# A one-core mLSTM and sparse-attention block: the compression's first layer in fp32r with its parts side by side, block-by-block scaling in the first and last attention unit, and decays formed a step earlier

## The chip, the core and the metric

The kernel runs on one core of a Trainium2 chip. The metric is the device time of one execution in microseconds (us). Smaller is better.

## The reference

One decoder layer works on 512 tokens of width 1024. A normalised x goes through one input projection of 8448 columns. Its columns feed an mLSTM branch (4 heads of 256) and a sparse attention branch (8 query heads of 64 in 2 key groups). The merged branches go through an output projection, a residual and a last norm. All inputs are fp32. What this change touches:

```python
p = _split_in(hN @ w_in[l])
# compression of keys and of values: 31 overlapping blocks of 32 tokens, 2 groups
def _compress(kv, pos_emb, w1, w2):
    blocks = kv[:, idx] + pos_emb[None, None, :, None, :]
    blocks = jnp.moveaxis(blocks, 3, 1).reshape(B, G, n_cmp, CMP_BLOCK * dk)   # (1, 2, 31, 2048)
    return jax.nn.gelu(blocks @ w1) @ w2                                       # w1 2048x128, w2 128x64
# attention, per block of 128 queries
p_c = jax.nn.softmax(jnp.where(m_c, s_c, NEG), axis=-1) * m_c        # against compressed keys
p_s = jax.nn.softmax(s_s, axis=-1)                                   # selected blocks
p_w = jax.nn.softmax(jnp.where(m_w, s_w, NEG), axis=-1)              # window
return g[..., 0:1] * o_c + g[..., 1:2] * o_s + g[..., 2:3] * o_w
# mLSTM, per head
s = jnp.einsum('bhld,bhsd->bhls', qc, kc) * jnp.exp(logD - m_t[..., None])
h = num / jnp.maximum(jnp.abs(den), jnp.exp(-m_t))[..., None]
...
x = x + merged @ w_out[l]
return _rmsnorm(x, final_norm_g)
```

With 512 tokens, 8 selection blocks and 16 chosen ones, every selection block is chosen, so both the selected and the window branch are plain causal attention with their own keys and values.

## The kernel before, in words

**Projections.** Each fp32 operand that goes into a large product is split into two fp32r parts, a high part `h` and a rest `l`, and three products replace one: h·h, l·h and h·l. For a weight panel of 128x1024 the load is `wr`, ScalarE (ACT) writes `wh`, VectorE (DVE) subtracts and writes `wl`. One projection job (`cols`) is 24 matmuls `pp<-hTh,wh`, `pp<-hTl,wh`, `pp<-hTh,wl` of 128x512: 8 blocks of the width by 3 products. `cols(NKC, ..., 2)` cuts one such job into two token halves of 128x256.

**The stream.** Jobs stand in a queue, `stream`. `stream.step(n)` issues the next n matmuls of it, `stream.run(n)` finishes n jobs, and each finished job calls its `post` function. Matmuls of the stream are what TensorE (PE) does between the steps of the other work; this text calls them fill. They have to be done at some time, so moving them from one place to another changes no total.

**What sets the order.** Each engine has one queue, in order. A list scheduler makes it from the order in which the code is written; where an engine's name is in the set `ordered`, the written order holds: ACT and DVE while the first attention query is prepared, PE at the beginning and the end of the kernel. Loads are issued by SyncE (SP) in its queue's order. A tile pool's buffer comes free when its last reader ends.

**Compression.** `blocks(i)` (i = 0 keys, 1 values) loads the 2048x128 weight into `w1t`, copies the projection to `Z` and forms `X`, the overlapping blocks with the position term added. `hidden(i)` multiplies: 16 products in plain fp32, each 128x128 of `w1t` with 128x64 of `X`. The trace shows two records for each. Then comes the gelu chain `u`, `u2`, and `compress_k`, `compress_v` multiply by the second weight `w2t` and leave `KC` (keys) and `VC` (values). The tiles of this stage lie in the pool `cmp`, over memory that earlier tiles used.

**Attention.** `rope_a` copies a projected query or key and turns it by DMA (`rot`); `rope_b` and `query_heads` finish it and leave the parts `Th`. There are 16 units: 4 query pairs c, 2 heads hh, 2 branches b. `score` makes `ps<-k,Th` for the query blocks qb = 0 to 3 of 128, 256, 384 and 512 columns; `softmax_block` negates and masks on DVE (a custom instruction that leaves the row extreme in `st`), and takes exp on ACT with the row sum. At qb = 3 one reciprocal of four columns is multiplied by the gates and GpSimd (POOL) scales the four blocks of `P`. Then `P` is transposed on PE (`pt<-cst,P`), split (`pth`, `ptl`) and multiplied with the values (`po`). `tick(FILL)` puts 3 fills behind each step, `START_FILL` 12 behind each of the first unit's. `compressed(c)` makes the scores against `KC`: `pp<-KC,rh`, softmax `sc`, transposes `pp<-cst,sc`.

**mLSTM.** For each of 4 heads: the decay matrix `Dm` starts from `ps<-ghl,sel` and seven exps on ACT; the scores `ps<-qkh,qkh` are multiplied into it, split into `Sh`, `Sl`, multiplied with the values into `num`, normalised, and transposed (`pt<-cst,num`) into `yah`. Before the transposes the stream goes on until the next head's key is projected; after the last head `NORM_FILL` 30 fills stand there.

**End.** The sums of squares of each block of 128 tokens collect in `fs`; `begin`, `more` and `factor` on POOL add them in `fb` and raise to the power -1/2.

Of the kernel before, what the change touches and what calls it, by code (L numbers as in the profile page):

```python
# [60 lines left out]
def build(  # L61
# [731 lines left out]

    def blocks(i):
        def post(ps):
            w1, w2 = ((cmp_w1_k, cmp_w2_k), (cmp_w1_v, cmp_w2_v))[i]
            nc.sync.dma_start(W1[i], w1[0].rearrange("(j q) h -> q j h", q=128))
# [12 lines left out]
            pool.memset(X[:, :, :, 31:32], 0.0)  # L810
            for g in range(2):
                zz = Z[:, g, :]
                zin = bass.AP(zz.tensor, zz.offset, [zz.ap[0], [1, 16], [8, 31]])
                dve.tensor_tensor(
                    X[:, :, g, 0:31], zin,
                    cpos[:, i * 16 : i * 16 + 16].unsqueeze(2).broadcast_to([128, 16, 31]), OP.add,
                )
# [428 lines left out]
    for h in range(4):  # L1246
        for i in range(2):
            for e in range(2):
                conv(i, h, e)
    for j in range(ND):  # L1250
        branch(GB, j, ybh, ybl, 4)
    stream.run(4)
    values(0)

    for h in range(4):
        (qh, ql), (kh, kl) = qk[0, h], qk[1, h]
        vh, vl = vv[h]
# [86 lines left out]
    with tc.tile_pool(name="fin", bufs=1, reuse_waits="tile") as fp:  # L1344
# [112 lines left out]
        def more(tb, n):  # L1457
            v = fb[:, tb : tb + 1]
            keep(pool.tensor_tensor(v, v, fs[:, tb, n : n + 1], OP.add))
# [138 lines left out]
```

## Time and profile before

| what | value |
|---|---|
| time, median of three runs | 612.02 us (611.96, 612.02, 612.77) |
| the profiled execution's own time | 612.24 us |
| its span, first to last instruction | 610.4 us |
| PE busy | 596.2 us, 98% |
| DVE busy | 483.1 us, 79% |
| ACT busy | 343.2 us, 56% |
| POOL busy | 63.4 us, 10% |

The span is what the trace covers; the execution's own time has 1.8 us around it. "Busy" is the time in which at least one instruction of that engine is in flight. Matmuls overlap: a 128x512 matmul has a record of 0.39 us, and the next starts about 0.23 us after it, so PE's busy share hides short waits that the distance between the starts of two matmuls shows. Places below are given in us from the start of the span.

### The profile page before, as it was taken

How to read it: one execution, taken by the hardware profiler on the slowest of the kernel's cores; microseconds unless marked ns; L12 is line 12 of the kernel's file. 1: busy time of each engine (PE TensorE's matmuls, PEld its weight loads, DVE VectorE, ACT ScalarE, POOL GpSimd, SP SyncE). 2: the span in 40 equal slices, each digit the busy share in tenths (PEclk: the TensorE clock that was granted, in tenths of full speed). 3: DMA queues.
4: the chain of work that ended last, by engine and by line, in shares of the span. 5: the costliest groups of instructions: out<-in, count | busy, mean ns of one | idle time of the engine just before them, and what ended most of it. 6: DMA issues, size and time to landing. Idle time of an engine off the chain costs nothing. (4 is left out here: it accounts for less than half of the span.)

```text
span 610.4 us, 8577 instructions
## 1 busy us (share of the span) xinstructions
PE 596.2 (98%) x3008; PEld 499.5 (82%) x3008; DVE 483.1 (79%) x906; ACT 343.2 (56%) x635; POOL 63.4 (10%) x126
## 2 busy tenths in 40 slices
PE   8999999999999999999999999999999999999995
PEld 6988888888888877888888887888788878888884
DVE  5879798696686578886977684889898997589984
ACT  6854646664442356665765674465756563434564
POOL 3000000000100003222122131000000000010122
PEclk9999999999999999999999999999999999999998
DMA  7966555302068361323313113422242234890633
GB/s 221 349 162 190 183 168 160 116 2 86 18 185 207 78 173 46 97 59 86 81 47 103 53 34 122 138 70 70 69 130 80 89 87 131 301 253 18 208 52 139
DMA packets 83637, 74.18 MB, mean 122 GB/s; under 512 B 5197, under 2 KB 65225, under 8 KB 83594
## 3 DMA queue, kind: packets, MB, share of 16 engines
q1 hardware_dynamic: 82296, 70.94, 39.1%
q0 software_dynamic: 1008, 2.36, 2.1%
q8 instruction: 24, 0.39, 0.3%
q10 hardware_dynamic: 290, 0.33, 0.2%
q14 instruction: 19, 0.16, 0.1%
HBM read 61.36 MB, written 8.45 MB: 114 GB/s over the span
## 5 line engine op out<-in xcount | busy, mean ns | idle before, releaser
L77 PE MATMUL pp<-hTh,wh 128*128 128x512 f32 (+1 forms) x360 | 143.8, 400 | 0.0
L77 PE MATMUL pp<-hTl,wh 128*128 128x512 f32 (+1 forms) x360 | 139.9, 389 | 0.0
L77 PE MATMUL pp<-hTh,wl 128*128 128x512 f32 (+1 forms) x360 | 139.5, 388 | 0.0
L77 ACT ACTIVATE wh<-wr 128x1024 fp32r<-128x1024 f32 x56 | 59.1, 1060 | 50.5 <-PE pp L77 44.6
L77 DVE TENSOR_TENSOR wl<-wr,wh 128x1024 fp32r<-128x1024 f32 x56 | 68.2, 1219 | 21.1 <-ACT wh L77 21.0
L77 PEld LDWEIGHTS pp<-hTh,wl 128*128 128x128 f32 x360 | 67.7, 188 | 13.1
L77 PEld LDWEIGHTS pp<-hTh,wh 128*128 128x128 f32 x360 | 67.9, 189 | 10.7
L77 PEld LDWEIGHTS pp<-hTl,wh 128*128 128x128 f32 x360 | 68.0, 189 | 9.4
L1055 POOL TENSOR_SCALAR P<-P,st 128x128 f32<-128x128 f32 (+1 forms) x64 | 38.1, 615 | 152.5 <-DVE st L77 134.4
L77 ACT ACTIVATE P<-P,st 128x128 f32<-128x128 f32 (+3 forms) x64 | 35.7, 558 | 22.1 <-DVE st L77 21.2
L77 DVE TENSOR_TENSOR ptl<-pt,pth 128x512 fp32r<-128x512 f32 (+1 forms) x64 | 30.9, 486 | 16.2 <-ACT pth L77 15.0
L77 DVE TENSOR_TENSOR wl<-T,wh 128x1024 fp32r<-128x1024 f32 x28 | 33.9, 1221 | 11.4 <-ACT wh L77 11.3
L77 DVE TENSOR_TENSOR wl<-R,wh 128x1024 fp32r<-128x1024 f32 x28 | 33.8, 1219 | 9.5 <-ACT wh L77 9.5
L77 ACT ACTIVATE wh<-T 128x1024 fp32r<-128x1024 f32 x28 | 29.4, 1057 | 18.4 <-PE pp L77 10.3
L77 ACT ACTIVATE pth<-pt 128x512 fp32r<-128x512 f32 (+1 forms) x64 | 27.2, 426 | 18.8 <-PE pt L77 18.4
L77 ACT ACTIVATE wh<-R 128x1024 fp32r<-128x1024 f32 x28 | 29.1, 1057 | 13.8 <-PE pp L77 6.7
L77 DVE SCALAR_TENSOR_TENSOR u<-pp,prm,u 128x511 f32<-128x511 f32 (+2 forms) x48 | 35.6, 742 | 0.4 <-ACT u L77 0.2
L77 DVE CUSTOM_DVE_ANT_0 P<-ps,cst 128x128 f32<-128x128 f32 (+3 forms) x64 | 30.5, 483 | 5.0 <-PE ps L77 4.8
L77 PE MATMUL pt<-cst,P 128*128 128x128 f32 x160 | 29.6, 275 | 2.7 <-POOL P L1055 2.5
L77 PE MATMUL ps<-k,Th 128*128 128x256 f32 (+2 forms) x112 | 29.0, 339 | 0.2 <-DVE st L77 0.2
L77 PEld LDWEIGHTS pt<-cst,P 128*128 128x128 f32 x160 | 20.7, 141 | 10.2 <-POOL P L1055 4.7
L77 PE MATMUL pp<-yah,wh 128*128 128x512 f32 x64 | 25.0, 391 | 0.0
(345 smaller groups left out, 1341.4 us busy)
## 6 DMA issues: line engine op xcount, KB each, us to landing
wr<-w_in SPq DMA_DIRECT2D x44, 512.0 KB
R<-w_in SPq DMA_DIRECT2D x24, 512.0 KB
gD<-sg SPq DMA_DIRECT2D x16, 256.0 KB
s<-gD SPq DMA_DIRECT2D x16, 256.0 KB
wr<-w_branch_a SPq DMA_DIRECT2D x8, 512.0 KB
R<-w_out SPq DMA_DIRECT2D x8, 512.0 KB
vD<-cq SPq DMA_DIRECT2D x8, 256.0 KB
wr<-vD SPq DMA_DIRECT2D x4, 512.0 KB
```

The source lines that it names most:

```text
L77: ins = fn(*args, **kw)
L1055: pool.tensor_scalar(pj, pj, st[:, 2, j : j + 1], 1.0, OP.mult, OP.mult)
```

## The change

1. `hidden(i)` now takes both operands as two fp32r parts that lie side by side: X[high, low] is the stationary 128x128 operand, W1[high, low] the moving one of 256 columns, so that 16 matmuls of 128x256 give all four products at once. `both` adds the two column halves (ACT copies one, DVE adds the other), and a small fp32 matmul with `twice` (two identities over each other) adds the row halves and turns the result. W1 and X have to be split: W1 arrives in two halves through the panel buffers `wr`, X in two halves `Xr`. W1 of the values is put in the memory of `yb`, which is not yet in use.
2. The first projection of the keys is no longer cut in two.
3. The compression's end (`compress_k`, `compress_v`) and the first query's rope stand ahead of the first attention step, with fill between.
4. In units 0 and 15 each block of `P` is scaled as soon as its exp is done: a reciprocal of one column on DVE, the product on POOL for qb 0 to 2, on DVE in two pieces (128 and 384 columns) for qb 3.
5. `START_FILL` is 7, `PRE_FILL` 20 new.
6. `decay(h + 1)` is written ahead of head h's last steps; 4 more fills (`NEXT_FILL`) stand ahead of the transposes of heads 0 to 2, and `NORM_FILL` is 36.
7. Two additions at the end go from POOL to DVE.

```diff
-START_FILL = 12
+START_FILL = 7
+PRE_FILL = 20
+EDGES = (0, 15)
-NORM_FILL = 30
+NORM_FILL = 36
+NEXT_FILL = 4
...
-    cols(NKC, lambda ps: blocks(0)(ps), 2)
+    cols(NKC, lambda ps: blocks(0)(ps))
...
+    W1 = [
+        cp.tile([128, 16, 2, 128], F32R, name="w1t"),
+        yb[:, : 8 * T].rearrange("p (j s h) -> p j s h", j=16, s=2),
+    ]
+    twice = cp.tile([128, 128], F32, name="twice")[:, :64]
+    dve.tensor_tensor(twice, ident[:, 0:64], ident[:, 64:128], OP.add)
+    def side_by_side(raw, t, js):
+        split(raw, t[:, js, 0, :], t[:, js, 1, :])
...
-            nc.sync.dma_start(W1[i], w1[0].rearrange("(j q) h -> q j h", q=128))
+            for js in halves_of_j:
+                raws.append(wp.tile([128, 8, 128], F32, name="wr", tag="wr", bufs=3))
+                src = w1[0].rearrange("(j q) h -> q j h", q=128)
+                nc.sync.dma_start(raws[-1], src[:, js])
...
-            X = cp.tile([128, 16, 2, 32], F32, name=f"X{i}")
+            X = cp.tile([128, 16, 2, 64], F32R, name=f"X{i}")
+            for n, js in enumerate(halves_of_j):
+                raw = rpp.tile([128, T], F32, name="Xr", tag=f"Th{n}")
...
+                side_by_side(raw.rearrange("p j g n -> p j (g n)"), X, js)
+            for raw, js in zip(raws, halves_of_j):
+                side_by_side(raw, W1[i], js)
...
             pe.matmul(
-                ph[:, :64], W1[i][:, j, :], Xs[i][:, j].rearrange("p g n -> p (g n)"),
-                start=j == 0, stop=j == 15,
+                ph[:, :256], Xs[i][:, j].rearrange("p s n -> p (s n)"),
+                W1[i][:, j].rearrange("p s h -> p (s h)"), start=j == 0, stop=j == 15,
             )
+        A(both, ph[:, 0:128], AF.Copy)
+        dve.tensor_tensor(both, ph[:, 128:256], both, OP.add)
+        return both
+    def activated(i, both):
+        ph = PS()
+        pe.matmul(ph[:, :64], both, twice, start=True, stop=True)
...
     u0 = hidden(0)
+    stream.step(16)
+    u0 = activated(0, u0)
     stream.run()
     keys(0, rope_b(*roped.pop(("k", 0))))
     u1 = hidden(1)
+    compress_k(u0)
+    stream.step(16)
+    u1 = activated(1, u1)
     stream.run()
     keys(1, rope_b(*roped.pop(("k", 1))))
+    compress_v(u1)
+    ordered.update(("act", "dve"))
+    first = query_turned(0)
     stream.step(4)
-    ordered.update(("act", "dve"))
-    query_heads(0)
-    compress_k(u0)
-    stream.step(14)
-    compress_v(u1)
+    query_heads(0, first)
+    stream.step(PRE_FILL)
...
+    def block_scaled(c, hh, b, qb, P, st):
+        g = (2 * c + hh) * 3 + 1 + b
+        r, gate_of = st[:, 2, qb : qb + 1], gates[:, qb, g : g + 1]
+        dve.reciprocal(r, st[:, 1, qb : qb + 1])
+        cut = 128 if qb == NT - 1 else 0
+        pj = P[:, POFF[qb] : POFF[qb] + (qb + 1) * 128]
+        for eng, part in ((dve, pj[:, :cut]), (dve if cut else pool, pj[:, cut:])):
+            if part.shape[1]:
+                eng.tensor_scalar(part, part, r, gate_of, OP.mult, OP.mult)
...
-        if qb == NT - 1:
+        if units.index((c, hh, b)) in EDGES:
+            for j in (0, 1) if qb == 1 else (qb,):
+                block_scaled(c, hh, b, j, P, st)
+        elif qb == NT - 1:
...
+    stream.run(2)
+    decay(0)
+    stream.run(2)
...
+            if tb == 3 and h < 3:
+                decay(h + 1)
             A(num[:, tb], po[:, :258], AF.Copy)
...
                 stream.step(1)
+            stream.step(NEXT_FILL)
...
         square(1, R0, 1)
+        factor(0, 1, dve)
         times(0, R)
-        factor(0, 1)
-        more(1, 1)
+        more(1, 1, dve)
```

What this does to the queues at four places follows, as the built programs order the instructions; line numbers are L77 before and L80 after because all go through one recording function.

DVE at the compression, before: two panels' rests (`wl`), then `Z` and `X` of the keys straight from the projection.

```order
L77 TENSOR_TENSOR wl_1695<-wr_1692,wh_1694 128x1024
L77 SCALAR_TENSOR_TENSOR zt_1298<-zt_1298,cq_1572 128x512
L77 SCALAR_TENSOR_TENSOR gate_80<-gate_80,zt_1298 128x512
L77 TENSOR_TENSOR wl_1738<-wr_1735,wh_1737 128x1024
L77 COPY Z0_1683<-pp_1631 64x256
L77 TENSOR_TENSOR X0_1688<-Z0_1683,prm_70 128x16x31
L77 COPY Z0_1683<-pp_1631 64x256
L77 TENSOR_TENSOR X0_1688<-Z0_1683,prm_70 128x16x31
```

DVE at the same place, after (`w1t` is the split weight of the keys, `yb` here holds that of the values, `Xr` the blocks in fp32).

```order
L80 TENSOR_TENSOR w1t_1604<-wr_1656,w1t_1604 128x8x128
L80 TENSOR_TENSOR w1t_1604<-wr_1658,w1t_1604 128x8x128
L80 COPY Z_1662<-pp_1631 64x256
L80 TENSOR_TENSOR wl_1687<-wr_1684,wh_1686 128x1024
L80 COPY Z_1662<-pp_1631 64x256
L80 TENSOR_TENSOR Xr_1668<-Z_1662,prm_70 128x8x31 x2
L80 TENSOR_TENSOR Xr_1674<-Z_1662,prm_70 128x8x31 x2
L80 TENSOR_TENSOR yb_1592<-wr_1715,yb_1592 128x8x128
L80 TENSOR_TENSOR X0_1667<-Xr_1668,X0_1667 128x8x64
L80 TENSOR_TENSOR X0_1667<-Xr_1674,X0_1667 128x8x64
```

Four weight splits and four `X` splits have come in over both compressions, and the first split of the values' weight stands ahead of the keys' `X`. One panel's rest (`wl_1695`) no longer stands ahead of the last `gate`.

DVE where the first query is prepared, before: `KC` stands behind the query's parts `Th`.

```order
L77 TENSOR_TENSOR Th_1937<-ra_1912,Th_1937 64x512
L77 TENSOR_TENSOR Th_1940<-ra_1912,Th_1940 64x512
L77 COPY KC0_1582<-ps_1943 64x32
L77 TENSOR_TENSOR sc_2017<-pp_2012,cst_69 128x256
L77 COPY KC1_1583<-ps_1943 64x32
```

DVE where `KC` stands after.

```order
L80 TENSOR_TENSOR both_1879<-ps_1862,both_1879 128x128
L80 COPY KC0_1582<-ps_1882 64x32
L80 TENSOR_TENSOR k01_1610<-ra_1780,k00_1609 64x512
L80 TENSOR_TENSOR k11_1612<-ra_1780,k10_1611 64x512
L80 COPY KC1_1583<-ps_1882 64x32
```

`KC` has moved up to right behind the values' `both`; the query's `Th` follows 18 rows behind these.

DVE at the first unit's softmax, before: the four-column reciprocal stands behind the fourth block of branch 0 and two other blocks.

```order
L77 ISA P,st<-ps,cst 128x512
L77 ISA st 128x1
L77 TENSOR_TENSOR mx<-mx,gates 128x8
L77 TENSOR_TENSOR sc<-sc,mx 128x256
L77 ISA P,st<-ps,cst 128x256
L77 ISA st 128x1
L77 TENSOR_TENSOR sc<-sc,cst 128x256
L77 RECIPROCAL st<-st 128x4
L77 ISA P,st<-ps,cst 128x384
L77 ISA st 128x1
L77 TENSOR_TENSOR st<-st,gates 128x4
```

The same place after.

```order
L80 RECIPROCAL st<-st 128x1
L80 ISA P,st<-ps,cst 128x256
L80 ISA st 128x1
L80 RECIPROCAL mx<-mx 128x8
L80 RECIPROCAL st<-st 128x1
L80 ISA P,st<-ps,cst 128x384
L80 ISA st 128x1
L80 TENSOR_TENSOR mx<-mx,gates 128x8
L80 TENSOR_SCALAR P<-P,st,gates 128x128
L80 TENSOR_TENSOR sc<-sc,mx 128x256
L80 TENSOR_SCALAR P<-P,st,gates 128x384
```

Each block has a reciprocal of its own in DVE's queue, and the largest block's scaling stands there too, in two pieces; POOL has three blocks of this unit instead of four.

ACT between the second and the third mLSTM head, before: the exps of the third head's `Dm` stand behind the second's transposed output `yah`.

```order
L77 ACTIVATE yah<-pt,prm 128x512 x2
L77 ACTIVATE th<-u 128x512
L77 ACTIVATE wh<-wr 128x1024
L77 ACTIVATE qkh_4542<-u 128x512
L77 ACTIVATE Dm<-dg,cs 128x128
L77 ACTIVATE Dm<-ps,cs 128x384
L77 ACTIVATE Dm<-dg,cs 128x128
L77 ACTIVATE Dm<-ps,cs 128x256
```

The same place after.

```order
L80 ACTIVATE num<-po 128x258
L80 ACTIVATE num<-pt 128x258
L80 ACTIVATE vh<-wr 128x4x256
L80 ACTIVATE th<-u 128x512
L80 ACTIVATE Dm<-dg,cs 128x128
L80 ACTIVATE Dm<-ps,cs 128x384
L80 ACTIVATE Dm<-dg,cs 128x128
L80 ACTIVATE Dm<-ps,cs 128x256
```

The exps have moved up to right behind the evacuation of `num`, ahead of the normalisation and of `yah`.

More of the change, by code (lines that the diff above doesn't have):

```diff
@@ L788, in build @@
     cp = cmp_pool.__enter__()
-    Xs, W1, W2, roped = [], [], [], {}
-    for i, (w1, w2) in enumerate(((cmp_w1_k, cmp_w2_k), (cmp_w1_v, cmp_w2_v))):
-        W1.append(cp.tile([128, 16, 128], F32, name=f"w1t{i}"))
+    Xs, W2, roped = [], [], {}
+    W1 = [
[4 more added lines that the diff above has]
+    dve.tensor_tensor(twice, ident[:, 0:64], ident[:, 64:128], OP.add)
+    for i in range(2):
         W2.append(cp.tile([128, 2, 64], F32, name=f"w2t{i}"))
+    halves_of_j = slice(0, 8), slice(8, 16)
+    def side_by_side(raw, t, js):
+        split(raw, t[:, js, 0, :], t[:, js, 1, :])
     def blocks(i):
@@ L808, in post @@
                         dve.tensor_copy(dst, src)
-            X = cp.tile([128, 16, 2, 32], F32, name=f"X{i}")
[L810 to L817, printed above, removed]
+            X = cp.tile([128, 16, 2, 64], F32R, name=f"X{i}")
+            for n, js in enumerate(halves_of_j):
+                raw = rpp.tile([128, T], F32, name="Xr", tag=f"Th{n}")
+                raw = raw.rearrange("p (j g n) -> p j g n", j=8, g=2)
+                pool.memset(raw[:, :, :, 31:32], 0.0)
+                for g in range(2):
+                    zz = Z[:, g, :]
+                    zin = bass.AP(zz.tensor, zz.offset + n * 8, [zz.ap[0], [1, 8], [8, 31]])
+                    pos = cpos[:, i * 16 + n * 8 : i * 16 + n * 8 + 8]
+                    dve.tensor_tensor(
+                        raw[:, :, g, 0:31], zin, pos.unsqueeze(2).broadcast_to([128, 8, 31]), OP.add
+                    )
+                side_by_side(raw.rearrange("p j g n -> p j (g n)"), X, js)
+            for raw, js in zip(raws, halves_of_j):
+                side_by_side(raw, W1[i], js)
             Xs.append(X)
@@ L878, in queries, with query_turned, query_heads @@
         cols(NQ + c * 128, post)
-    def query_heads(c):
+    def query_turned(c):
         raw, rot, a = roped.pop(("q", c))
-        q = rope_b(raw, rot, a)
+        return raw, rope_b(raw, rot, a)
+    def query_heads(c, turned=None):
+        raw, q = turned or query_turned(c)
         Th = []
@@ L1244, in branch, with decay @@
         stream.add(load, gen)
[L1246 to L1257, printed above, removed]
+    decayed = {}
+    def decay(h):
         pgb = PS()
@@ L1272, in build @@
                 A(Dm[:, o + 128 : o + n], pgb[:, (sb + 1) * 128 :], AF.Exp, bias=bias, scale=-1.0)
+        decayed[h] = Dm
+    for h in range(4):
+        for i in range(2):
+            for e in range(2):
+                conv(i, h, e)
+    for j in range(ND):
+        branch(GB, j, ybh, ybl, 4)
+    stream.run(2)
+    decay(0)
+    stream.run(2)
+    values(0)
+    for h in range(4):
+        (qh, ql), (kh, kl) = qk[0, h], qk[1, h]
+        vh, vl = vv[h]
+        Dm = decayed.pop(h)
         Sh = mp.tile([128, 1280], F32R, name="Sh", tag="Sh")
@@ L1455, in begin, with more, factor @@
             keep(pool.tensor_scalar(fb[:, tb : tb + 1], fs[:, tb, 0:1], EPS, None, OP.add))
-        def more(tb, n):
+        def more(tb, n, eng=None):
             v = fb[:, tb : tb + 1]
-            keep(pool.tensor_tensor(v, v, fs[:, tb, n : n + 1], OP.add))
-        def factor(tb, n):
-            more(tb, n)
+            keep((eng or pool).tensor_tensor(v, v, fs[:, tb, n : n + 1], OP.add))
+        def factor(tb, n, eng=None):
+            more(tb, n, eng)
             keep(pool.tensor_tensor(fr[:, tb : tb + 1], fb[:, tb : tb + 1], mhalf[:, 0:1], OP.pow))
```

10 lines of the change are left out of this document (6 added, 4 removed).

## The prediction, made before the changed kernel had run

> **What bounds the kernel now.** I read the busy shares first, then PE's waits, then PE's own rows around the places that the diff touches.
>
> ```profile
> PE 596.2 (98%) x3008; PEld 499.5 (82%) x3008; DVE 483.1 (79%) x906; ACT 343.2 (56%) x635; POOL 63.4 (10%) x126
> ```
>
> PE is the bound in nearly all of the span, so a change pays in two ways: PE work that goes, and waits of PE that go. Fill that is moved pays nothing by itself. PE's waits for other engines, over the whole span (total us, times, longest):
>
> ```profile
> PE pt L77 <- POOL P L1055: 2.5, 5, 1.0
> ...
> PE pt L77 <- DVE num L77: 1.1, 2, 0.6
> ...
> PE pp L77 <- DVE KC L77: 0.4, 1, 0.4
> PE ps L77 <- ACT qkh L77: 0.3, 1, 0.3
> ```
>
> These four are what parts 3 to 6 of the change address: the scaling at the attention's edges, the compressed keys, and the mLSTM heads. They are only 4.3 us, but a listed wait understates its loss: a matmul's record goes on after the next could have started. I therefore take the distance of starts less the usual distance.
>
> **The compression's PE work.** The timeline of PE:
>
> ```profile
> 175.77 0.28 PE L77 MATMUL pp<-hTh,wh 128*128 128x256 f32 x1
> 175.89 0.28 PE L77 MATMUL pp<-hTl,wh 128*128 128x256 f32 x1
> ...
> 189.69 0.39 PE L77 MATMUL pp<-hTh,wl 128*128 128x512 f32 x1
> 189.92 3.68 PE L77 MATMUL ps<-X,w1t 128*128 128x64 f32 x32
> 193.40 0.48 PE L77 MATMUL pp<-hTh,wh 128*128 128x512 f32 x1
> ...
> 208.94 0.33 PE L77 MATMUL ps<-u,w2t 128*128 128x64 f32 x2
> ...
> 209.39 0.40 PE L77 MATMUL pp<-hTh,wl 128*128 128x512 f32 x1
> ...
> L77 PE MATMUL ps<-X,w1t x64: 217/275/275, 189.9 to 202.4; 128*128 128x64 f32 x64
> ```
>
> The last row, of the tile view, counts 64 records in both hidden layers, two for each product. One layer takes 193.40 - 189.92 = 3.48 us, and the other has the same 32 records: 6.96 us go. A 128x256 fp32r matmul with a new weight each time follows its predecessor after 0.12 us, so 16 of them are 1.92 us, twice 3.84. The two `twice` products are fp32, 128x64, like the row at 208.94: from there to 209.39 less one fill of 0.227 is 0.22 us, two make 0.44. The first projection in one piece is 24 x 0.227 = 5.45 for 48 x 0.12 = 5.76, which is 0.3 less. PE's work: -6.96 + 3.84 + 0.44 - 0.3 = **-3.0 us**. Its bounds are -2.1, if going into and out of each new chain costs another 0.22 like that row (four times), and -3.2, if `twice` costs half of it.
>
> The Trainium skill speaks against this term: "FP8 and Floating Point Precision" (TensorE Precision Notes) counts four passes for a true fp32 product, and by "TensorE: Matmul & The Clock Gate" (Back-to-back issue gap) a column takes 1/2.4 GHz. Estimated from the two pages, 16 products of 4 x 64 columns take 1.7 us, as long as 16 of 256 columns in one pass. The trace does not agree for the old form, with 3.48 us, or 0.109 us for each of 32 records.
>
> **What hides the new splits.** DVE now makes four halves of W1 and four of X, plus `both`. The rows that price them and the stage's room (windows: length, then PE, PEld, DVE, ACT, POOL busy):
>
> ```profile
> 178.04 0.69 DVE L77 SCALAR_TENSOR_TENSOR gate<-gate,zt 128x512 f32<-128x512 f32 x1
> 180.23 1.23 DVE L77 TENSOR_TENSOR wl<-wr,wh 128x1024 fp32r<-128x1024 f32 x1 [1.50 <-ACT wh L77]
> ...
> 183.55 1.12 DVE L77 TENSOR_TENSOR X<-Z,prm 128x496 f32<-128x496 f32 x1
> ...
> 178.88 0.87 SPq L797 DMA_DIRECT2D w1t<-cmp_w_k  x1
> ...
> 184.50:189.90 5.40, 5.40 (x25) 4.48 (x24) 4.40 (x6) 1.78 (x4) 0.00 (x0) 1.00 1.10 282
> 189.90:198.90 9.00, 9.00 (x57) 8.04 (x56) 4.42 (x10) 2.12 (x4) 0.00 (x0) 1.00 0.57 139
> ```
>
> Four W1 halves at 1.22 and four X halves at 0.69 (the 128x512 row) are 7.6 us, on a DVE that has 5.6 us free in these two windows and idles 1.50 ahead of the `wl` at 180.23. That is nearly all of its room, and what does not fit moves to later work. ACT, busy 3.9 of 14.4, has room for its copies of the same tiles. Everything hangs on `X` being ready when PE has done the 24 + 24 fills between: PE is through the keys' projection at 178.70 and needs `X` 48 x 0.227 later, at 189.6. DVE's queue after the last `gate` (which has one `wl` less ahead of it, so it ends about 177.8 instead of 178.73) holds two W1 splits, two `Z`, a `wl`, four half additions at 0.57, one more W1 split and two X splits: 2.4 + 0.9 + 1.2 + 2.3 + 1.2 + 1.3 = 9.3 us, plus gaps of about 0.7 for ACT. That is 187.8, a slack of 1.8 us. The second `X` comes to 194.5 against a need at 197.2. `both` has 16 fills, 3.6 us, for an ACT copy and a DVE addition behind an in-order queue; it comes within 0.3 us of its need. I charge **+0.3** (0 to +2: beyond the slack, each us of lateness is one of PE).
>
> SP: two loads instead of one per weight, at 0.87 us of issue, through the panel buffers ahead of the next panel. Before, the loads could issue only at 178.88, when the pool's memory was free; the panel buffers come free earlier, so the keys' weight lands ahead of the last `gate`. The ropes' and keys' DMAs keep their number; `query_turned` is written earlier but its DMAs were issued in `rope_a` before. The values' weight in `yb` waits for nothing, since `yb` is first written when the first query pair's units are done. Cost 0.
>
> **The attention's beginning.** Rows of PE, DVE and POOL:
>
> ```profile
> 219.45 0.39 PE L77 MATMUL pp<-hTh,wl 128*128 128x512 f32 x1
> 220.24 1.10 PE L77 MATMUL pp<-KC,rh 128*128 128x64 f32 x8 [0.40 <-DVE KC L77]
> ...
> 223.65 0.39 PE L77 MATMUL pp<-hTh,wh 128*128 128x512 f32 x1
> 224.29 0.48 PE L77 MATMUL ps<-k,Th 128*128 128x256 f32 x2 [0.24 <-DVE st L77]
> ...
> 230.07 0.60 PE L77 MATMUL pp<-cst,sc 128*64 128x128 f32 x4
> 231.66 0.33 PE L77 MATMUL pt<-cst,P 128*128 128x128 f32 x1 [0.99 <-POOL P L1055]
> ...
> 229.38 0.17 DVE L77 RECIPROCAL st<-st 128x4 f32<-128x4 f32 x1
> ...
> 230.48 2.81 POOL L1055 TENSOR_SCALAR P<-P,st 128x128 f32<-128x128 f32 x4 [51.39 <-DVE st L77]
> ```
>
> The losses are 0.79 - 0.23 = 0.56, 0.64 - 0.23 = 0.41 and 1.59 - 0.44 = 1.15; with the two short breaks behind the last it is about 3.0 us. In the new order `KC` stands twenty rows ahead of `Th` in DVE's queue, so the first goes. POOL's 2.81 us chain starts only after the last block's exp; now three blocks are scaled while later scores run, and the last takes a reciprocal of 0.17 and two DVE pieces of about 0.29 and 0.55 (the custom instructions of these sizes). Late next is that last block, 0.55, then `sc` on the same DVE, 0.3, and short breaks around the two small compression products, 0.45: 1.3 remain. I take **-1.7** (-2.8 if all cover holds; +0.5 if DVE, whose new reciprocals each wait for an exp of 0.4 to 0.7 us in order, delays the next blocks). The `PRE_FILL` matmuls are cover only: without them the 9 us of rope, split and copies would be open.
>
> The Trainium skill ("SBUF — State Buffer", Who interferes with whom) has a rule against this: a DVE instruction with two SBUF inputs locks out GpSimd's reads. The row at 603.10 below agrees; if the scaling on POOL met that in every block, it would cost up to 3 x 0.5 us, which still is under the 2.81 us that POOL no longer has at the end.
>
> **The attention's end.** Here unit 15 has no unit behind it.
>
> ```profile
> 367.06 0.28 PE L77 MATMUL po<-ptl,vsw 128*128 128x256 f32 x1
> 368.02 0.78 PE L77 MATMUL pt<-cst,P 128*128 128x128 f32 x2 [0.69 <-POOL P L1055]
> ...
> 366.79 2.86 POOL L1055 TENSOR_SCALAR P<-P,st 128x128 f32<-128x128 f32 x4 [4.76 <-PE po L77]
> ...
> 361.00:373.00 12.00, 10.48 (x57) 7.84 (x55) 7.90 (x21) 6.58 (x18) 3.89 (x5) 1.00 0.37 110
> ```
>
> PE idles 1.52 us of these twelve, and summed over its 57 rows the starts lose 3.6 us. POOL's chain of 2.86 us is again cut to the last block, on DVE. Left are the split `pth`, `ptl` and the free banks, some 2.2 us by the order: **-1.4** (-3.0 to 0).
>
> **mLSTM.** A window, and two of the waits:
>
> ```profile
> 424.00:434.00 10.00, 9.93 (x48) 7.89 (x47) 10.00 (x17) 5.63 (x10) 0.00 (x0) 1.00 0.36 105
> ...
> 434.56 0.56 ACT L77 ACTIVATE Dm<-ps,cs 128x384 f32<-128x384 f32 x1
> 435.02 0.62 ACT L77 ACTIVATE qkh<-u 128x512 fp32r<-128x512 f32 x1
> ...
> 435.70 0.50 PE L77 MATMUL ps<-qkh,qkh 128*128 128x512 f32 x1 [0.26 <-ACT qkh L77]
> ...
> 458.73 0.39 PE L77 MATMUL pp<-hTl,wh 128*128 128x512 f32 x1
> 459.61 0.30 PE L77 MATMUL pt<-cst,num 128*128 128x128 f32 x1 [0.50 <-DVE num L77]
> ```
>
> The starts lose 0.65 at the transposes of two heads, 0.53 and 0.35 at one head's `qkh`, and short pieces: 2.6 us over four heads. Four more fills are 0.9 us of cover for `num`, more than the 0.65. With `Dm` formed earlier, `qkh` no longer stands behind its exps. But DVE is full for ten microseconds at a stretch (10.00 of 10.00 in the window), and the fills only move PE ahead of a DVE that is no faster; the wait may come back at the next head. I take about half, **-1.4** (-2.4 to 0).
>
> **The end.**
>
> ```profile
> 603.10 0.69 POOL L1459 TENSOR_TENSOR fb<-fb,fs 128x1 f32<-128x1 f32 x1 [2.22 <-ACT junk L77]
> ...
> 604.39 0.19 POOL L1459 TENSOR_TENSOR fb<-fb,fs 128x1 f32<-128x1 f32 x1
> 604.61 0.48 DVE L77 CUSTOM_DVE_ANT_0 junk<-xo,fb 128x256 f32<-128x256 f32 x1 [0.53 <-POOL fb L1459]
> ```
>
> The same addition takes 0.69 us at 603.10 and 0.19 at 604.39. On DVE both leave POOL's chain, which the last reduction waits for by 0.53: **-0.3** (-0.5 to 0).
>
> **Sum.** -3.0 + 0.3 - 1.7 - 1.4 - 1.4 - 0.3 = -7.5 us, from the profiled execution's own 612.24 to 604.7; the median of the runs is 0.2 lower, so **604.6** against 612.02.
>
> **Rivals.**
> - *The edges give nothing* (0.17): the one-column reciprocals wait in DVE's queue for ACT, and what POOL no longer delays, DVE does. For it: in the new order each of them stands ahead of the next block's custom instruction. Against: POOL's 2.8 us chain is the listed wait. 604.6 + 3.1 = 607.7.
> - *The heads stay DVE's* (0.15): the full window speaks for it, the ACT row ahead of `qkh` against. 606.0.
> - *All named waits go* (0.13): the cover is there on paper at each. -3.0 - 3.0 - 3.0 - 2.4 - 0.4 is 600.4, with a rest of short breaks about 601.5.
> - *The splits come late* (0.08): the slack of 1.8 us is used up by ACT's W1 copies, +2: 606.6.
> - *No PE work is saved in the hidden layers* (0.02): if the new 128x256 products, with 64 columns of each part, took as long as the pairs of records that they replace, only the rest would stay: 604.6 + 3.1 = 607.7. The 0.12 us of 128x256 fill against 0.218 for a pair speaks against it. The Trainium skill's two pages named above would come out so.
> - *Slower* (0.03): the first half of the values' weight is split ahead of the keys' `X` in the queues of both DVE and ACT. If that load, behind four small `w2t` loads on SP, lands late, `X` is late with it and PE stands. In the sum above that split begins at about 185.3; to decide, it must begin past 185.3 + 1.8 + 7.5 = 194.6. The panel split at 180.23 waited only 1.50. The time is then above 613.2.
> - A smaller lateness of that load, one that eats 6.3 to 8.7 of the 7.5 us, ends within 0.2% (1.2 us, about what a measurement of this kernel tells from no change): 0.03.
>
> The forecast keeps 0.39. The range of 8 in 10 reaches from the third rival to beyond the first: 601.3 to 608.4. Faster 0.94, same 0.03, slower 0.03.
>
> **What would show it.** Right: PE's rows `ps` from `X` and `w1t` of 128x256 last under 2.1 us each and follow a fill without a wait; no wait of `pp` for `KC`; waits of `pt` for POOL's `P` under 0.5 us at the edges; no wait for `num` over 0.3. Wrong: PE waits for `X` or `both` by more than 1 us, or waits of PE for DVE's `P` or `ptl` as large as POOL's were.

## The result, and the profile after

The changed kernel takes 608.14 us (median of four runs, 607.67 to 608.39) against 612.32 us of the kernel before on the same chip: a ratio of 0.9927, 95% interval 0.9915 to 0.9939. That is 4.2 us less, where 7.5 had been forecast; the range held it by 0.3 us. The profiled execution took 607.67 us with a span of 605.9.

The busy shares of the page after:

```profile
PE 592.9 (98%) x2956; PEld 495.7 (82%) x2956; DVE 494.4 (82%) x931; ACT 350.5 (58%) x645; POOL 63.0 (10%) x124
```

PE's busy time went down by 3.3 us and DVE's went up by 11. PE's waits after (total, times, longest):

```profile
PE pt L80 <- DVE num L80: 1.9, 2, 0.9
...
PE po L80 <- DVE ptl L80: 1.2, 2, 1.0
PE ps L80 <- DVE both L80: 1.0, 1, 1.0
PE pp L80 <- DVE cs L80: 0.3, 1, 0.3
```

Every wait that the change was aimed at in the attention is gone: no line for POOL's `P`, none for `KC`. In their place stand four lines for DVE, of which only `num` was there before, and it has grown from 1.1 to 1.9. (A wait of 1.3 us for DVE's `zero` stands in both kernels.) Where the time went can be read stage by stage.

**Compression.** PE's timeline, and those of ACT and DVE ahead of the product with `twice`:

```profile
189.47 2.08 PE L80 MATMUL ps<-w1t,X 128*128 128x256 f32 x16
191.38 0.40 PE L80 MATMUL pp<-hTh,wh 128*128 128x512 f32 x1
...
194.81 0.39 PE L80 MATMUL pp<-hTh,wh 128*128 128x512 f32 x1
196.19 0.43 PE L80 MATMUL ps<-twice,both 128*128 128x64 f32 x2 [1.00 <-DVE both L80]
...
198.37 2.08 PE L80 MATMUL ps<-yb,X 128*128 128x256 f32 x16
200.28 0.33 PE L80 MATMUL ps<-u,w2t 128*128 128x64 f32 x2
...
194.13 1.05 ACT L80 ACTIVATE wh<-wr 128x1024 fp32r<-128x1024 f32 x1
195.08 0.27 ACT L80 ACTIVATE both<-ps 128x128 f32<-128x128 f32 x1
...
193.90 1.32 DVE L80 TENSOR_TENSOR X<-Xr,X 128x512 fp32r<-128x512 f32 x2
195.25 0.69 DVE L80 TENSOR_TENSOR ra<-pp,Ct 128x512 f32<-128x512 f32 x1
195.86 0.28 DVE L80 TENSOR_TENSOR both<-ps,both 128x128 f32<-128x128 f32 x1
```

Each hidden layer lasts 1.91 us (191.38 - 189.47, 200.28 - 198.37) where it lasted 3.48, and both follow a fill without a wait. But `both`, 0.27 us of ACT and 0.28 of DVE, could have started at about 191.5. ACT starts its copy at 195.08, behind a panel's `wh`, and is done at 195.35. DVE comes to the addition only at 195.86: its queue runs without a gap through the splits of the values' `X` and a rope product, `ra`. The distance of PE's starts from 194.81 to 196.19 is 1.16 us above that of a fill.

**The attention's beginning and end.** PE at the first scores, and two windows (length, PE, PEld, DVE, ACT, POOL busy), the first over the beginning, the second over the end:

```profile
215.59 0.39 PE L80 MATMUL pp<-hTh,wl 128*128 128x512 f32 x1
215.81 0.64 PE L80 MATMUL ps<-k,Th 128*128 128x256 f32 x4
...
214.00:228.00 14.00, 14.00 (x76) 11.79 (x76) 12.83 (x38) 9.01 (x24) 1.69 (x3) 1.00 0.58 162
...
357.00:369.00 12.00, 12.00 (x69) 9.67 (x68) 9.31 (x23) 7.26 (x17) 1.21 (x2) 1.00 0.34 104
```

PE idled 1.52 us of the twelve at the end before and not at all now; at the beginning all five losses (0.56, 0.41, 1.15, 0.15, 0.45) are gone.

**Units 1 to 12.** The windows of the first unit and from 233 to 300 us of the kernel before; then the second of them of the changed one, and the largest wait in it:

```profile
219.00:233.00 14.00, 12.13 (x60) 8.90 (x59) 11.92 (x38) 9.24 (x27) 2.52 (x4) 1.00 0.39 111
233.00:300.00 67.00, 67.00 (x375) 56.57 (x374) 54.45 (x147) 43.50 (x111) 17.00 (x29) 1.00 0.27 74
```

```profile
233.00:300.00 67.00, 65.59 (x360) 54.59 (x361) 53.14 (x137) 41.87 (x103) 15.26 (x24) 1.00 0.25 70
...
243.98 0.40 PE L80 MATMUL pp<-hTl,wh 128*128 128x512 f32 x1
245.34 0.39 PE L80 MATMUL po<-ptl,vsw 128*128 128x256 f32 x1 [0.97 <-DVE ptl L80]
...
242.44 2.06 DVE L80 TENSOR_TENSOR Th<-ra,Th 64x512 fp32r<-64x512 f32 x2
...
244.87 0.41 DVE L80 TENSOR_TENSOR ptl<-pt,pth 128x256 fp32r<-128x256 f32 x1
...
240.51 3.46 POOL L1109 TENSOR_SCALAR P<-P,st 128x128 f32<-128x128 f32 x4 [7.63 <-ACT wh L80]
```

PE was busy in all of the longer stretch before; now it idles 1.41 us of it. DVE was busy 11.92 of 14 us in the first unit already. At 243.98 PE loses 1.14 us, and `ptl`, which it waits for, stands behind the two `Th` of the next query in DVE's queue. Over units 1 to 12, seven losses of 0.14 us and more add up to 2.9 us. The kernel before has none of that size there, and one of 0.18 a little further on, which the changed kernel has not: +2.7 between them.

**mLSTM.** ACT's evacuation of `num`'s last block in the second head, of the kernel before, then of the changed one with PE's wait behind it:

```profile
448.48 0.39 ACT L77 ACTIVATE num<-pt 128x258 f32<-128x258 f32 x1 [2.10 <-PE pt L77]
```

```profile
444.20 0.39 ACT L80 ACTIVATE num<-pt 128x258 f32<-128x258 f32 x1 [2.42 <-PE pt L80]
...
453.99 0.39 PE L80 MATMUL pp<-hTh,wl 128*128 128x512 f32 x1
455.32 0.30 PE L80 MATMUL pt<-cst,num 128*128 128x128 f32 x1 [0.94 <-DVE num L80]
```

From this evacuation to the transposes it takes 11.1 us in both (459.61 - 448.48 and 455.32 - 444.20). But the loss of PE there is 1.11 us where it was 0.66, and 1.08 in the third head where it was 0.73.

**The end.** The last reduction no longer waits for POOL:

```profile
599.52 0.15 DVE L80 TENSOR_TENSOR fb<-fb,fs 128x1 f32<-128x1 f32 x1
...
600.04 0.48 DVE L80 CUSTOM_DVE_ANT_0 junk<-xo,fb 128x256 f32<-128x256 f32 x1
```

### The profile page after: what moved, and what is told of

The parts are those of the page before. It is cut to its first block, busy times and chain, and to the rows that moved or that the text cites. A ratio compares the mean times of both kernels' runs of the same rounds, so it can differ in the third digit from the quotient of the medians.

```text
span 605.9 us, 8492 instructions
## 1 busy us (share of the span) xinstructions
PE 592.9 (98%) x2956; PEld 495.7 (82%) x2956; DVE 494.4 (82%) x931; ACT 350.5 (58%) x645; POOL 63.0 (10%) x124
## 4 chain that ended last, share of the span: by engine, by line
PE 82%; DVE 9%; ACT 4%; DMA 2%; issue 1%; POOL 1%; SPq 0%; ACTq 0%; POOLq 0%; DVEq 0%
PE pp L80 48%; PE ps L80 19%; PE pt L80 11%; PE po L80 4%; DVE wl L80 2%; ACT wh L80 1%; DMA xt<-x 1%; DMA wr<-cmp_w_v 1%; POOL rlr L125 1%; DVE xo L80 1%; ACT Dm L80 1%; DVE u L80 1%; DVE ptl L80 1%; DVE P L80 0%; DVE ra L80 0%
## 5 line engine op out<-in xcount | busy, mean ns | idle before, releaser
L80 PE MATMUL pp<-hTl,wh 128*128 128x512 f32 x352 | 142.6, 405 | 0.0
L80 PE MATMUL pp<-hTh,wh 128*128 128x512 f32 x352 | 138.7, 394 | 0.0
L80 PE MATMUL pp<-hTh,wl 128*128 128x512 f32 x352 | 138.3, 393 | 0.0
L80 ACT ACTIVATE wh<-wr 128x1024 fp32r<-128x1024 f32 x56 | 59.0, 1059 | 43.0 <-PE pp L80 33.0
L80 DVE TENSOR_TENSOR wl<-wr,wh 128x1024 fp32r<-128x1024 f32 x56 | 70.1, 1253 | 9.8 <-ACT wh L80 9.6
L80 PEld LDWEIGHTS pp<-hTh,wh 128*128 128x128 f32 x352 | 66.2, 188 | 13.3
L80 PEld LDWEIGHTS pp<-hTl,wh 128*128 128x128 f32 x352 | 66.2, 188 | 10.6
L80 PEld LDWEIGHTS pp<-hTh,wl 128*128 128x128 f32 x352 | 66.4, 189 | 9.9
L80 ACT ACTIVATE P<-P,st 128x128 f32<-128x128 f32 (+3 forms) x64 | 35.6, 557 | 26.0 <-DVE st L80 25.8
L80 DVE TENSOR_TENSOR wl<-T,wh 128x1024 fp32r<-128x1024 f32 x28 | 33.9, 1221 | 12.0 <-ACT wh L80 11.9
L1109 POOL TENSOR_SCALAR P<-P,st 128x128 f32<-128x128 f32 (+3 forms) x56 | 33.0, 609 | 100.2 <-DVE st L80 70.1
L80 DVE TENSOR_TENSOR wl<-R,wh 128x1024 fp32r<-128x1024 f32 x28 | 33.8, 1219 | 10.5 <-ACT wh L80 10.5
L80 DVE TENSOR_TENSOR ptl<-pt,pth 128x512 fp32r<-128x512 f32 (+1 forms) x64 | 30.8, 486 | 13.4 <-ACT pth L80 12.8
L80 ACT ACTIVATE wh<-T 128x1024 fp32r<-128x1024 f32 x28 | 29.4, 1056 | 18.8 <-PE pp L80 11.5
L80 ACT ACTIVATE pth<-pt 128x512 fp32r<-128x512 f32 (+1 forms) x64 | 27.5, 430 | 18.5 <-PE pt L80 17.9
L80 ACT ACTIVATE wh<-R 128x1024 fp32r<-128x1024 f32 x28 | 29.1, 1056 | 14.9 <-PE pp L80 6.2
L80 DVE SCALAR_TENSOR_TENSOR u<-pp,prm,u 128x511 f32<-128x511 f32 (+2 forms) x48 | 35.7, 743 | 1.3 <-ACT u L80 1.1
L80 DVE CUSTOM_DVE_ANT_0 P<-ps,cst 128x128 f32<-128x128 f32 (+3 forms) x64 | 30.4, 483 | 4.4 <-PE ps L80 4.1
L80 PE MATMUL ps<-k,Th 128*128 128x256 f32 (+2 forms) x112 | 28.5, 336 | 0.0
L80 PE MATMUL pt<-cst,P 128*128 128x128 f32 x160 | 28.2, 273 | 0.0
L80 PEld LDWEIGHTS pt<-cst,P 128*128 128x128 f32 x160 | 20.6, 142 | 6.4 <-DVE ptl L80 0.3
L80 PE MATMUL pp<-yah,wh 128*128 128x512 f32 x64 | 25.0, 391 | 0.0
```

The lines of the kernel that those rows point to most:

```text
L80: ins = fn(*args, **kw)
L1109: pool.tensor_scalar(pj, pj, st[:, 2, j : j + 1], 1.0, OP.mult, OP.mult)
```

## The experiments

The first 24 us of an execution, in which the inputs arrive, differed by up to 1.2 us between the profiled executions, whatever the kernel. So beside each time the table has the stretch from the last eight `pp<-slo,hTh` to the last matmul, which leaves them out. It also leaves out what follows the last matmul, 6.9 to 7.9 us in these traces. It is read from two rows of each trace; for the kernel before and the changed one they are

```profile
23.83 1.23 PE L77 MATMUL pp<-slo,hTh 128*128 128x288 f32 x8
...
603.16 0.28 PE L77 MATMUL pp<-wh,mSl 128*128 128x256 f32 x1
```

```profile
23.78 1.23 PE L80 MATMUL pp<-slo,hTh 128*128 128x288 f32 x8
...
598.95 0.28 PE L80 MATMUL pp<-wh,mSl 128*128 128x256 f32 x1
```

which is 579.33 and 575.17 us: 4.16 less, where the medians say 4.18.

| kernel | median us | before there, us | ratio (95% interval) | stretch us |
|---|---|---|---|---|
| before | | 612.32 | 1 | 579.33 |
| changed | 608.14 | 612.32 | 0.9927 (0.9915 to 0.9939) | 575.17 |
| e5: compression alone | 610.53 | 612.81 | 0.9967 (0.9954 to 0.9980) | 577.36 |
| e3: no scaling by block | 609.29 | 612.21 | 0.9960 (0.9947 to 0.9973) | 576.65 |
| e9: fill moved to units 1 and 2 | 604.94 | 612.21 | 0.9881 (0.9867 to 0.9896) | 572.06 |
| e11: e9 without scaling by block | 608.06 | 612.81 | 0.9922 (0.9907 to 0.9937) | 574.80 |
| e8: fill moved ahead of the heads' transposes | 606.46 | 612.21 | 0.9910 (0.9893 to 0.9926) | 573.66 |
| e7: decay behind rho | 609.50 | 612.21 | 0.9956 (0.9941 to 0.9971) | 576.88 |
| e6: `both` needed later | 606.88 | 612.81 | 0.9909 (0.9894 to 0.9924) | 574.70 |
| e10: e9, e8 and e6 together | 604.11 | 612.81 | 0.9858 (0.9842 to 0.9875) | 570.49 |
| e12: e10, compressed keys later | 603.00 | 612.14 | 0.9850 (0.9835 to 0.9864) | 569.72 |
| e13: e12 with the decay as before | 601.99 | 612.14 | 0.9839 (0.9822 to 0.9855) | 569.70 |

**e3, no scaling by block.**

```diff
-EDGES = (0, 15)
+EDGES = ()
```

> Against the changed kernel (608.1): no unit is scaled block by block, units 0 and 15 go back to one reciprocal and four blocks on POOL. Theory (this scaling removed the waits at both edges): the waits of PE for POOL's P come back, about 1.7 us at the beginning (the two that were 1.15 and 0.53) and 2.5 to 3.0 at the end: 612.0 to 612.8. Rival 1 (at the beginning the fill put ahead and the earlier compressed keys did it): only the end comes back, 610.6 to 611.1. Rival 2 (reciprocals in DVE's in-order queue cost as much as they bring): 607.5 to 609.

Measured: 609.29 us, 1.2 more than the changed kernel by the medians, 1.5 by the stretch. PE's waits:

```profile
PE pt L80 <- DVE num L80: 1.9, 2, 0.9
PE pt L80 <- POOL P L1109: 1.5, 3, 1.1
...
PE po L80 <- DVE ptl L80: 0.2, 1, 0.2
```

By the distance of starts, 1.2 us come back at the beginning and 1.9 more are lost at the end, 3.1 together. But the 1.14 us at 244 us and the 0.46 ahead of it are gone, and units 1 to 12 lose 1.9 us less in all; 1.0 us stays there. The kernel with the scaling by block gets through its first unit faster and then waits for DVE. The time hit none of the three expectations, because none had a term for the units between.

**e9, one more fill behind each score step of units 1 and 2**, eight in all, which the last unit no longer has.

```diff
-        tick(FILL - 1 if 3 * last // 4 <= n < last else FILL)
+        tick(FILL - 1 if 3 * last // 4 <= n < last else FILL + (n < 3 * NT))
```

> Against the changed kernel (608.1): 4 fills instead of 3 behind each score step of units 1 and 2, so 8 fills (1.8 us) go from the last unit to these two. The changed kernel's new waits in units 1 to 3 add up to about 2 us by starts, the largest 1.14 at 244 us, for DVE's ptl. Theory (DVE carries work over from the compression and PE runs ahead of it): the waits in units 1 to 3 fall below 0.8 us, the last unit loses up to 1.8 us; net 606.5 to 608.5. Rival (the wait is made at one place, where the rest of a panel and two parts Th stand ahead of ptl in DVE's queue while POOL scales): it stays above 1 us, and the time is 608.5 to 610.

Measured: 604.94 us, 3.2 less than the changed kernel, more than either theory expected. The same two windows, and a row of DVE:

```profile
233.00:300.00 67.00, 67.00 (x374) 56.69 (x373) 54.53 (x144) 44.80 (x110) 15.00 (x25) 1.00 0.24 68
361.00:373.00 12.00, 12.00 (x62) 9.64 (x62) 7.95 (x17) 5.73 (x11) 0.05 (x2) 1.00 0.33 103
...
242.19 1.47 DVE L80 TENSOR_TENSOR Th<-ra,Th 64x512 fp32r<-64x512 f32 x2
```

PE is full again in both. Of the seven losses in units 1 to 12, 2.9 us together, none above 0.11 is left, and the last unit, with 8 fills less, loses 0.15 at one place. The rival, a wait made at one place by the two `Th` and POOL, is out as it was put: the two `Th` still stand ahead of that `ptl`, at 242.19, POOL scales beside them from 242.32, and PE does not wait. What was missing is time for DVE. The two `Th` also took 0.59 us less here than in the changed kernel (1.47 for 2.06); how much of the gain that is, no run separates.

**e11, e9 without the scaling by block**

> The run with 4 fills in units 1 and 2 (604.9), and no unit scaled block by block. With 3 fills, taking the scaling away cost only 1.2 us: 3.1 came back at the edges and 1.9 went in units 1 to 3. Theory (the edges' gain was given back in units 1 to 3 because DVE had no time there): with the fill there, taking the scaling away costs its whole 3 us: 607.6 to 608.2. Rival (the scaling is worth only 1.2 us): 605.8 to 606.4.

Measured: 608.06 us, as the theory said, and a ratio of 0.9922 where e9 has 0.9881: 2.5 us slower by the ratios, 2.74 by the stretch. So the scaling is worth 2.5 to 2.7 us when DVE has cover in units 1 and 2, and only 1.2 to 1.5 (e3) when it has not. The rest of its gain was what the changed kernel gave back.

**e5, the compression alone**: the changed compression and its place ahead of the attention, and the rest as before.

```diff
-START_FILL = 7
-PRE_FILL = 20
-EDGES = (0, 15)
-NORM_FILL = 36
-NEXT_FILL = 4
+START_FILL = 12
+PRE_FILL = 0
+EDGES = ()
+NORM_FILL = 30
+NEXT_FILL = 0
...
-            if tb == 3 and h < 3:
-                decay(h + 1)
...
-        Dm = decayed.pop(h)
+        decay(h)
+        Dm = decayed.pop(h)
...
-        factor(0, 1, dve)
         times(0, R)
-        more(1, 1, dve)
+        factor(0, 1)
+        more(1, 1)
```

> The compression alone (parts 1 to 3 of the change with START_FILL 12), the rest as before (612.2): no scaling by block, the decay at the head of its own head, NEXT_FILL 0, NORM_FILL 30, the end as before. Theory (the hidden layers save 3.0 us of PE, PE waits 1.2 us for both, KC no longer comes late, 0.6; the waits of units 1 to 3 in the changed kernel come from the shorter first unit and not from the compression's splits): the rest as before, 609.8. Rival (DVE's 8 us of splits are carried into the attention and PE waits for them there): the waits for ptl and sc of 1.5 to 2.5 us in units 1 to 3 are there too: 611.3 to 612.3.

Measured: 610.53 us where before took 612.81, 2.3 less (2.0 by the stretch). The waits:

```profile
PE ps L80 <- DVE both L80: 1.4, 1, 1.4
PE pt L80 <- POOL P L1109: 1.3, 2, 1.1
...
PE po L80 <- DVE ptl L80: 0.2, 1, 0.2
```

The theory stands in the main: the compression alone does not make the large waits that follow the first unit. But units 1 to 12 lose 1.1 us here by starts, in four breaks of 0.13 to 0.40, where the kernel before has none of that size. So about 1.0 of the 2.9 us that the changed kernel loses there come with the compression alone, and the other 1.9 with the scaling by block (e3 keeps 1.0 there too). Its own wait for `both` is a little longer here, 1.52 us by starts, and takes half of the 3.0 us that PE saves.

**e6, the first `both` needed later**

```diff
-    stream.step(16)
+    stream.step(22)
     u0 = activated(0, u0)
...
     u1 = hidden(1)
+    stream.step(10)
     compress_k(u0)
-    stream.step(16)
+    stream.step(6)
```

> Against the changed kernel (608.1): 22 fills instead of 16 between the first hidden layer and the product with twice, and 10 of the 16 fills behind the second hidden layer ahead of the compressed keys' product. Theory (both is 1.4 us late in ACT's and DVE's queues, and nobody else is late by it): the wait of 1.2 us goes, 606.9. Rival (the queues are full, what follows both is as late): a wait of about 1 us at the keys' second layer or at the second both, 608.0.

Measured: 606.88 us, as the theory said, and yet the trace speaks for the rival: the wait for `both` is gone, and a new one stands at the keys' second layer, 0.90 us by starts.

```profile
PE ps L80 <- DVE u L80: 0.7, 1, 0.7
```

The stretch is only 0.47 us shorter; of the rest of the 1.2 us, 0.36 lie in the beginning of the two profiled executions (23.42 us for 23.78), and the other 0.4 are within the spread of the runs.

**e8, fill moved ahead of the transposes of the mLSTM heads**

```diff
-NEXT_FILL = 4
+NEXT_FILL = 12
...
             dve.scalar_tensor_tensor(yal[:, ct], pt, w, f(yah[:, ct]), OP.mult, OP.subtract)
-            stream.step(6)
+            stream.step(2)
```

> Against the changed kernel (608.1): the fills behind each of the two transposes of an mLSTM head go from 6 to 2 and those ahead of them (NEXT_FILL) from 4 to 12. The order then has 66, 50, 50 and 38 fills between a head's last value product and its transposes, instead of 60, 44, 44 and 38, and the next head's scores follow after as many fills as before. Theory (too little fill ahead of the transposes: the chain from the last value product to the normalised num takes 11.1 us in both kernels, and 44 fills cover 10.0): both waits of PE for num go, 1.1 us each by the distance of starts, so 606.0 (605.5 to 606.5). Rival (DVE is the limit, the wait only moves): 607.7 to 608.5, with waits for qkh or for ps of about 2 us in their place.

Measured: 606.46 us, 1.7 less. Both waits for `num`, 2.2 us by starts, are gone, and one of 0.50 has come for `qkl`:

```profile
PE ps L80 <- DVE qkl L80: 0.3, 1, 0.3
```

The theory of too little fill holds.

**e7, the decay behind rho**

```diff
-            if tb == 3 and h < 3:
-                decay(h + 1)
...
         A(rho, num[:, :, 256], AF.Abs)
+        if h < 3:
+            decay(h + 1)
```

> Against the changed kernel (608.1): the next head's decay is written behind rho, the first step of a head's normalisation on ACT, instead of ahead of the last evacuation of num; the fills ahead of the transposes become 58, 42, 42 and 38. Theory A (the seven exps, 2.9 us of ACT, and DVE's 0.7 stand ahead of rho and lengthen the chain to num): the chain from the last evacuation of num to the transposes falls from 11.1 us to about 9, both waits for num go, 606.5, less if qkh does not come late. Theory B (the chain is set by DVE's queue, and only the number of fills ahead matters): the chain stays near 11.1 and each of two waits grows by 2 fills, 0.45 us: 609.0.

Measured: 609.50 us, 1.4 more. Each theory was right in one half. With two fills less ahead of the transposes there is no wait for `num` above 0.2 us: in the second head it takes at most 9.6 us from the evacuation at 445.41 to the transposes at 455.00, where it took 11.1. So the exps ahead of `rho` had lengthened that chain. But PE now waits at the next head's scores, 2.5 us by starts:

```profile
PE ps L80 <- ACT qkh L80: 2.2, 2, 1.1
...
460.15 0.49 PE L80 MATMUL ps<-qkh,qkh 128*128 128x512 f32 x1 [1.10 <-ACT qkh L80]
```

Work on ACT that goes ahead of one chain of the head comes out of the other.

**e10, e9, e8 and e6 together**

> The changed kernel with the three moves of fill together: 4 fills in units 1 and 2, 12 ahead of the heads' transposes and 2 behind each, 22 ahead of the first product with twice. Theory (each move removes a wait of its own): 608.1 - 3.2 - 1.7 - 1.2 = 602.0, up to 602.8 if the small waits for qkl stay. Rival (the waits return where fill was taken): 604 to 605.

Measured: 604.11 us, 8.7 less than before there, and inside the range of the rival. The stretch is 4.7 us shorter than the changed kernel's, where 6.1 had been expected. The 6.1 were summed from medians, e6's 1.2 among them; by the stretch the three moves alone had brought 3.11, 1.51 and 0.47, or 5.1 us, and 0.4 of these are missing. The wait for the first `u`, 0.88 us, is there as in e6.

**e12, the compressed keys' product behind the second `twice`, and e13, the same with the decay as before the change**

```diff
     u1 = hidden(1)
-    stream.step(10)
-    compress_k(u0)
-    stream.step(6)
+    stream.step(16)
     u1 = activated(1, u1)
+    compress_k(u0)
```

> The run with all three moves of fill, but the compressed keys' product stands behind the second product with twice, 6 fills later. In that run PE waited 0.9 us (by starts) for the first u there. Theory (u0 takes 5.5 us from its twice product, and nothing else is late): the wait goes; against before on the same chip the ratio falls from 0.986 to 0.984 to 0.985, about 8.7 + 0.9 = 9.6 us under before. Rival (the second both or the second u is late now): as the run before it, 0.986.

> The kernel of the run beside it, with each head's decay at the head of its own head as before the change. The fills ahead of the transposes stay 66, 50, 50 and 38. Theory (the early decay takes the exps away from ahead of qkh; it pays once the fills cover num): PE's waits for qkh come back, 0.6 to 2.0 us over four heads, that much slower than the run beside it. Rival (the early decay brings nothing; only the fill ahead of the transposes counts): within 0.3 us of it.

Measured: 603.00 and 601.99 us, ratios 0.9850 and 0.9839. Of e12's expected 0.9 us, 0.77 came by the stretch; 0.43 us of the wait for `u` are left. The rows of the stretch, of e12 and then of e13:

```profile
24.60 1.23 PE L80 MATMUL pp<-slo,hTh 128*128 128x288 f32 x8
...
594.32 0.28 PE L80 MATMUL pp<-wh,mSl 128*128 128x256 f32 x1
```

```profile
PE ps L80 <- ACT qkh L80: 0.9, 2, 0.7
...
23.49 1.23 PE L80 MATMUL pp<-slo,hTh 128*128 128x288 f32 x8
...
593.19 0.28 PE L80 MATMUL pp<-wh,mSl 128*128 128x256 f32 x1
```

569.72 and 569.70 us: the same. The two profiled executions are 2.05 us apart (603.96 and 601.91), 1.11 of it ahead of the stretch (24.60 against 23.49) and 0.89 behind the last matmul (7.85 against 6.96). So the 1.0 us between the medians need not come from the decay; what made it is open. With the decay as before, PE's waits for `qkh` come back (0.82 and 0.40 us by starts), but those for `qkl` and at the first scores go (0.51 and 0.21), and other short breaks make up the rest. The rival holds by the stretch: with enough fill the early decay brings nothing that can be measured. Both kernels have a stretch 5.4 us shorter than the changed one's.

## Why the prediction came out as it did

The terms, as forecast and as the two traces have them by the distance of starts:

| term | forecast | measured |
|---|---|---|
| PE's work in the compression | -3.0 | -3.0 |
| the splits come in time, `both` | +0.3 | +1.2 |
| attention's beginning | -1.7 | -2.7 |
| units 1 to 12, with the 0.18 behind them | no term | +2.7 |
| attention's end | -1.4 | -2.4 |
| mLSTM | -1.4 | +0.35 |
| end of the kernel | -0.3 | -0.35 |
| sum | -7.5 | -4.2 |

The stretch and what follows the last matmul are 4.5 us less together (4.16 and 0.34); the table does not place the other 0.3.

- **PE's work** was right to 0.1: -6.96 + 3.82 + two `twice` + the first projection in one piece. The rival that priced products by columns is out: 16 products of 128x256 take 1.91 us, where 32 fp32 records of 64 columns took 3.48. By an estimate from the Trainium skill's "FP8 and Floating Point Precision" (TensorE Precision Notes) with "TensorE: Matmul & The Clock Gate" (Back-to-back issue gap) the two would have been alike; the trace decides against it.
- **The splits**: the first `X` was done at 188.4 against a forecast of 187.8, and PE asked for it at 189.47. The step that failed is "it comes within 0.3 us of its need" for `both`. It never added what stands ahead of `both` on DVE: the splits of the values' `X`, which it had ending at 194.5, and a rope product of 0.69. By its own numbers the addition would have been done at about 195.5, 0.4 us after the fills ran out (195.04). DVE's queue came 0.7 later still, with `X` done at 195.22: it had waited 1.2 us for ACT's copies, where 0.7 had been allowed. So the addition was done at 196.14, 1.1 us late. ACT came to its own copy 3.5 us late too, behind two `X` copies, a rope copy and a panel's `wh`, but was done 0.5 us before DVE reached the addition, so DVE's queue set the wait. The forecast had also counted 7.6 us of new splits for 5.6 us free and 1.5 idle on DVE, and gave the overflow no price.
- **The edges**: the mechanism was right, and the terms were mis-sized the other way; the waits for POOL went entirely, near the bound that "if all cover holds" gave for the beginning. The rival that the edges give nothing is out (e11: 2.5 to 2.7 us).
- **What is late next** was asked for each place by itself, and so the step that failed most is that the sum has no term for units 1 to 12. DVE's queue carries the same work in a stretch that PE now reaches earlier, and e3 and e9 show it from both sides: without the scaling by block 1.9 of the 2.9 us of losses there go, and with 8 more fills there all of them go. The other 1.0 us come with the compression (e5). DVE's 11.92 busy us of 14 at the beginning could have been read from the trace of before, and the forecast read the windows of DVE for the compression and the heads alone.
- **mLSTM**: the step that failed is "four more fills are 0.9 us of cover for `num`". The loop ahead of `NEXT_FILL` runs the stream up to a fixed job (the next head's key), so fills that one head takes more are missing at the next. The order had 54, 47, 45 and 36 fills between the last value product and the transposes before, and has 60, 44, 44 and 38 now: more only in the first and the last head, which had no wait. Three fills less and one less are 0.7 and 0.2 us, and the losses grew by 0.45 and 0.35. e8, which takes the fills from behind the transposes, removed them. The second half of that step, that `qkh` no longer stands behind the exps, was right, and was paid for at `rho` (e7, e13).
- **Signs to look for**: the two hidden layers under 2.1 us without a wait, no wait for `KC`, none for POOL's `P` at the edges, came out right; "no wait for `num` over 0.3" was wrong, and two signs of error that had been named occurred: PE waits for `both` by more than 1 us, and a wait for `ptl`, 1.0 us, is as long as POOL's longest was.
- **Small slips**: 612.02 less 7.5 is 604.5 and not 604.6, and the 600.4 of the third rival counts from the profiled execution. The losses at the attention's beginning, summed to "about 3.0", are 2.7 by the same distances.

The likeliest case was thus not the one that happened. Two gains larger than forecast, a loss that was not in the sum and a gain that did not come happened together. The time came out next to the 607.7 of two rivals, and the mechanisms of both are out. That it stayed inside the range is in part luck: the edges gained 2.0 us more than forecast and so hid most of the 2.7 us for which the sum had no term.

## What to carry to other kernels

A wait that is removed ahead of an engine with little time to spare comes back at the next place that needs this engine; list what is late next over the whole stretch until that engine idles again, and move cover there (8 matmuls from the last unit to units 1 and 2 were worth 3.2 us here, about as much as the new multiplication). Fill is a fixed budget: if a loop runs it to a fixed job, more of it at one step is taken from the next, so count it in the order at every step before crediting it. When a small step has to pass a full queue, sum what stands ahead of it there: here 0.28 us of work came 1.1 us late.

## What the runs showed of the hardware

POOL's four blocks of scaling took 2.06 us at 250.54, where only the last of them met two-input work of DVE out of SBUF (a `wl`, which took 1.63 us there instead of 1.22), and 3.46 us beside a `wl` and the two `Th` at 240.51. The reciprocal square root of 128x4 took 1.92 us beside a `wl`, and 1.01 beside a `u` in the kernel before. Rows of the changed kernel, then two of the kernel before:

```profile
250.54 2.06 POOL L1109 TENSOR_SCALAR P<-P,st 128x128 f32<-128x128 f32 x4 [6.58 <-DVE st L80]
...
451.35 1.92 POOL L125 TENSOR_TENSOR rlr<-va,prm 128x4 f32<-128x4 f32 x1 [6.89 <-DVE va L80]
```

```profile
218.55 1.40 DVE L77 TENSOR_TENSOR Th<-ra,Th 64x512 fp32r<-64x512 f32 x2 [0.70 <-ACT Th L77]
...
456.60 1.01 POOL L122 TENSOR_TENSOR rlr<-va,prm 128x4 f32<-128x4 f32 x1 [7.87 <-DVE va L77]
```

It goes both ways: the two `Th` at 242.44, while POOL was scaling, took 2.06 us on DVE, where such a pair took 1.40 with POOL idle at 218.55 in the kernel before. Which side loses more is not fixed: in e9 the pair at 242.19 took 1.47 us and the first two of POOL's four blocks 0.79 and 0.91, where at 250.54 they took 0.38 and 0.48. The Trainium skill ("SBUF — State Buffer", Who interferes with whom) states that a DVE instruction with two SBUF inputs contends with a GpSimd instruction that reads SBUF; these rows agree. No run took this contention away by itself, so what it costs the whole kernel stays open.
